# Seven block products for eight in a feed-forward up projection on TensorE

## The chip, the cores and the metric

The kernel runs on one core of a Trainium2 chip. The metric is device time in microseconds for one execution, as the median over runs. One profiled execution of the kernel before is read here. Its engines are TensorE (PE in the profile, with its weight loads as PEld), VectorE (DVE), ScalarE (ACT), GpSimd (POOL) and SyncE (SP), which only issues transfers.

## What is computed

Two transformer blocks over 1024 tokens of width 1024, in float32. The change lies in the feed-forward part of the first block, where D_FF is 2816:

```
def causal_dwconv(x, w):
    ...
    xp = jnp.pad(x, ((0, 0), (k - 1, 0), (0, 0)))
    out = xp[:, 0:t] * w[0]
    for i in range(1, k):
        out = out + xp[:, i:i + t] * w[i]
    return out

def conv_glu_ffn(h, w_up, conv_w, w_down):
    up = causal_dwconv(h @ w_up, conv_w)
    gate, val = jnp.split(up, 2, axis=-1)
    return (jax.nn.silu(gate) * val) @ w_down
...
        h = rms_norm(x, ffn_norm_g[l])
        x = x + conv_glu_ffn(h, w_up[l], ffn_conv_w[l], w_down[l])
```

So the up projection is a product of 1024 tokens x 1024 by 1024 x 5632 (2816 gate columns, then 2816 value columns), a convolution of three taps along the tokens follows, and the gated values go through a 2816 x 1024 down projection.

## The kernel before

A float32 product is made of three passes on TensorE: each operand is split into a rounded high part and a low part (`split`: ACT casts the high part at L101, DVE subtracts it at L102), and `mm3` (L124) adds high x high, high x low and low x high. Tokens lie along the free axis in two halves of 512, since one PSUM bank holds 128 x 512 floats.

**Ahead of the up projection**, `out_unit` (L960 to L964) makes 128 tokens x 512 columns of x per unit, and `Norm` normalizes each 128-token row group: `put` (L165 to L185) scales it, `turn` (L194) transposes it on PE and splits it into `hh` and `hl`, the two parts of the transposed activations. One turn is done behind each following unit, and the last one stands behind the last unit.

**The up projection** runs over 22 units `fi`. A unit is one block of 128 gate columns and one of 128 value columns. For each, `wload` brings a 1024 x 128 block of weights (`wraw`, 512 KB, SP queue) and splits it into `whi` and `wlo`; `mm3` makes 8 k-tiles x 3 passes x 2 token halves = 48 matmuls of 128x512 into `mm`, a tile of two banks, of which there are two. `up_evict` applies the convolution straight from PSUM: ACT scales (L1044), DVE adds the two shifted taps (L1045, L1046). Then ACT takes tanh (L1066), DVE makes `th` (L1067) and the gated product (L1071) in two halves, which stay in SBUF in the tiles `gg`. In unit 20 the first row of `w_down` and `gg[0][0]` are split ahead into `down0` (L1072 to L1080).

**The down projection** (L1149 to L1180) has four groups (token half j, column half c). Each runs over the 22 rows fi of `w_down`: SP loads `wr` (256 KB), ACT and DVE split it and the matching `gg` half, and PE makes 12 matmuls into four accumulators.

Instructions run on each engine in a fixed order that a scheduler lays down when the program is built: it takes what is ready by its estimate, and `high_priority` moves splits ahead. At run time each engine works through its list in order, and waits on semaphores.

Of the kernel before, what the change touches and what calls it, by code (L numbers as in the profile page):

```python
# [8 lines left out]
F32 = mybir.dt.float32  # L9
# [57 lines left out]
def kernel(ctx: ExitStack, tc: tile.TileContext, A: dict, out: bass.AP, stop=None):  # L67
# [129 lines left out]


# [4 lines left out]
    mmp = stw.enter_context(tc.tile_pool(name="mmp", bufs=2, space=PSUM))  # L203
# [724 lines left out]
    st1.close()  # L928

# [71 lines left out]
    def block2_tables(pool):  # L1001
# [3 lines left out]
        for c in range(3):  # L1005
# [30 lines left out]
        tc.keep_in_program_order(V.tensor_scalar(gq[:, 1:2], PV("qn_gain"), -(96.0 ** -0.5), None, op0=ALU.mult))  # L1036

    gg = []
    std0 = ExitStack()
    with tc.tile_pool(name="up", bufs=1) as up:  # L1040
        def up_evict(ps, ci):
            a = up.tile([128, T], F32, name="cv", bufs=3)
            w = [PV("ffn_conv_w", 2 * NF * i + ci) for i in range(3)]
            S.activation(a, ps, AF.Copy, scale=w[2])  # L1044
            V.scalar_tensor_tensor(a[:, 1:T], ps[:, 0:T - 1], w[1], a[:, 1:T], op0=ALU.mult, op1=ALU.add)  # L1045
            V.scalar_tensor_tensor(a[:, 2:T], ps[:, 0:T - 2], w[0], a[:, 2:T], op0=ALU.mult, op1=ALU.add)  # L1046
            return a
# [697 lines left out]
```

## Time and profile before

| | us |
|---|---|
| median of 3 runs | 2501.16 |
| lowest, highest | 2499.43, 2503.86 |
| the profiled execution, time | 2500.26 |
| the profiled execution, span | 2498.2 |

The span is what the profile covers; 2.06 us of the profiled execution's time lie outside it. The page gives the busy time of each engine; the windows of the trace give the same by stage, with TensorE's granted clock as a share of its full rate (1.00 is 2.4 GHz, 0.50 is 1.2 GHz); the chain of waits tells what the end of a stretch hung on.

### The profile page before, as it was taken

To read this page: it belongs to the slowest core of one execution; us is meant where nothing else is said; L and a number is where in the kernel's file an instruction comes from. 1 tells how busy PE (TensorE), PEld (TensorE's weight loads), DVE (VectorE), ACT (ScalarE), POOL (GpSimd) and SP (SyncE) were. 2 spreads that over 40 slices of the span, in tenths; PEclk is the share of its full clock that TensorE was granted. 3 is DMA by queue.
4 is the path that set the end of the run, shared out by engine and by line. 5 is a ranking of instruction groups with operands and counts; after the bars stand their busy time and mean duration, and the time that the engine had idled before them with its cause. 6 is when DMAs were issued, how large, how long until landed. Compare 5 with 4: busy or idle time off the path is not lost.

```text
span 2498.2 us, 31184 instructions
## 1 busy us (share of the span) xinstructions
PE 2401.9 (96%) x11582; PEld 1941.4 (78%) x11582; DVE 1310.4 (52%) x2247; ACT 993.0 (40%) x1869; POOL 356.9 (14%) x477
## 2 busy tenths in 40 slices
PE   6999899999999989999999999999999999999999
PEld 5887676777777767788788888888789787787787
DVE  4245754578454333444444444556665534767852
ACT  4344333322333223322222222345556634669840
POOL 0122310013232211000000000001013200126510
PEclk9999999999999999999999999999999999999999
DMA  5322115353232355611111111334532556766433
GB/s 159 93 89 79 55 55 171 133 164 121 87 110 77 116 166 175 203 64 51 45 51 51 51 43 47 123 97 135 163 118 85 147 182 178 194 184 180 128 106 137
DMA packets 272055, 288.10 MB, mean 115 GB/s; under 512 B 13968, under 2 KB 208160, under 8 KB 271904
## 3 DMA queue, kind: packets, MB, share of 16 engines
q1 hardware_dynamic: 233056, 245.81, 32.8%
q10 hardware_dynamic: 38848, 40.31, 4.8%
q8 instruction: 91, 1.49, 0.2%
q14 instruction: 60, 0.49, 0.1%
HBM read 207.31 MB, written 78.75 MB: 115 GB/s over the span
## 4 chain that ended last, share of the span: by engine, by line
PE 46%; DMA 6%; ACT 4%; DVE 3%; issue 2%; SPq 0%; POOLq 0%; ACTq 0%; POOL 0%; DVEq 0%
PE mm L124 19%; PE ip L1230 3%; DMA mr<-merged 1%; DMA wr<-in_w_in_dram 1%; PE ip L1119 1%; PE ip L1120 1%; PE ip L1121 1%; PE iq L315 1%; PE tp L331 1%; PE iq L316 1%; PE lt L1514 1%; ACT p L1518 1%; DMA zr<-in_w_in_dram 1%; PE ip L962 1%; PE ip L960 1%
## 5 line engine op out<-in xcount | busy, mean ns | idle before, releaser
L101 ACT CAST whi<-wraw 128x1024 fp32r<-128x1024 f32 (+1 forms) x138 | 121.7, 883 | 505.5 <-PE mm L124 472.1
L102 DVE TENSOR_TENSOR wlo<-wraw,whi 128x1024 fp32r<-128x1024 f32 (+1 forms) x138 | 141.8, 1031 | 330.6 <-ACT whi L101 324.2
L124 PE MATMUL mm<-hh,whi 128*128 128x512 f32 x896 | 306.7, 414 | 7.6 <-ACT th L857 6.7
L124 PE MATMUL mm<-hh,wlo 128*128 128x512 f32 x896 | 292.0, 397 | 1.3 <-DVE wlo L116 1.3
L124 PE MATMUL mm<-hl,whi 128*128 128x512 f32 x896 | 291.5, 397 | 0.0
L124 PE MATMUL mm<-h2l,whi 128*128 128x512 f32 x704 | 222.4, 389 | 0.0
L124 PE MATMUL mm<-h2h,wlo 128*128 128x512 f32 x704 | 222.1, 389 | 0.0
L124 PE MATMUL mm<-h2h,whi 128*128 128x512 f32 x704 | 222.0, 389 | 0.0
L124 PEld LDWEIGHTS mm<-hh,wlo 128*128 128x128 f32 x896 | 170.0, 190 | 41.1 <-issue 2.5
L124 PEld LDWEIGHTS mm<-hl,whi 128*128 128x128 f32 x896 | 169.1, 190 | 36.8 <-DVE hl L102 0.4
L124 PEld LDWEIGHTS mm<-hh,whi 128*128 128x128 f32 x896 | 158.6, 191 | 44.8 <-ACT th L857 8.8
L124 PEld LDWEIGHTS mm<-h2l,whi 128*128 128x128 f32 x704 | 132.1, 188 | 28.6 <-issue 1.3
L124 PEld LDWEIGHTS mm<-h2h,whi 128*128 128x128 f32 x704 | 132.1, 188 | 28.1 <-ACT whi L101 0.6
L124 PEld LDWEIGHTS mm<-h2h,wlo 128*128 128x128 f32 x704 | 132.1, 188 | 27.4
L168 POOL TENSOR_TENSOR rs<-rs,negh 128x1 f32<-128x1 f32 x32 | 19.5, 610 | 869.1 <-ACT junk L165 603.1
L1518 ACT ACTIVATE p<-p,mn 128x640 f32<-128x640 f32 (+7 forms) x128 | 99.4, 778 | 12.2 <-DVE mn L1516 11.7
L102 DVE TENSOR_TENSOR ptl<-tp,pth 128x512 fp32r<-128x512 f32 (+3 forms) x144 | 78.0, 555 | 31.6 <-ACT pth L101 30.3
L102 DVE TENSOR_TENSOR gl<-s,gh 128x512 fp32r<-128x512 f32 x87 | 60.0, 690 | 64.6 <-ACT gh L101 62.1
L101 ACT CAST gh<-s 128x512 fp32r<-128x512 f32 x87 | 53.9, 621 | 78.7 <-PE iq L1177 32.7
L101 ACT CAST pth<-tp 128x512 fp32r<-128x512 f32 (+3 forms) x144 | 67.0, 477 | 42.5 <-PE tp L331 41.2
L315 PE MATMUL iq<-pth,v 128*128 128x512 f32 x192 | 70.7, 370 | 9.2 <-DVE t L1543 4.5
L867 POOL TENSOR_TENSOR acc<-acc,pacc 128x1024 f32<-128x1024 f32 x20 | 50.8, 2539 | 184.9 <-DVE acc L862 156.2
(508 smaller groups left out, 5223.5 us busy)
## 6 DMA issues: line engine op xcount, KB each, us to landing
wraw<-in_w_in_dram SPq DMA_DIRECT2D x60, 512.0 KB, 3.9
wraw<-in_w_up_dram SPq DMA_DIRECT2D x44, 512.0 KB, 3.8
wr<-in_w_down_dram SPq DMA_DIRECT2D x87, 256.0 KB, 2.6
merged<-acc SPq DMA_DIRECT2D x28, 512.0 KB, 3.0
pacc<-merged SPq DMA_DIRECT2D x20, 512.0 KB, 4.3
x<-x ACTq DMA_DIRECT2D x16, 512.0 KB, 3.0
v2t<-vo ACTq DMA_DIRECT2D x16, 512.0 KB, 2.6
v<-v2t SPq DMA_DIRECT2D x16, 512.0 KB, 4.0
```

The lines of the kernel that those rows point to most:

```text
L101: S.copy(hi, src)
L102: (eng or V).tensor_tensor(lo, src, f(hi), op=ALU.subtract)
L124: PE.matmul(ps[:, c0 + j * 512:c0 + (j + 1) * 512], w[:, k, :], x[j][:, k, :], start=(k == 0 and w is wh and x is xh), stop=(k == nkt - 1 ...
L315: PE.matmul(po[-1][:, w], vh[:, k, :], ph_[:, w], start=(k == 0), stop=False)
L316: PE.matmul(po[-1][:, w], vh[:, k, :], pl_[:, w], start=False, stop=(k == nk - 1))
L331: PE.transpose(pt[:, i * 128:(i + 1) * 128], P[p0 + i][:, k * 128:(k + 1) * 128], ident)
L867: G.tensor_tensor(ac, ac, pa, op=ALU.add)
L960: PE.matmul(po, mh[:, k, :], wh, start=(k == 0), stop=False)
L962: PE.matmul(po, ml[:, k, :], wh, start=False, stop=(k == NK - 1))
L1119: PE.matmul(ps[:, :ncol], xh[:, k, :], wh[:, :ncol], start=(k == 0), stop=False)
L1230: PE.matmul(ps[j], w[:, k, :], x[j][:, n, :], start=(n == 0 and w is wh and x is hh), stop=(n == 7 and bool(last)))
L1518: S.activation(pr_[:, :L], pr_[:, :L], AF.Exp, scale=-1.0, bias=mn[:, c:c + 1], accum_out=self.den[:, i:i + 1])
```

## The change

The up projection's product is cut into blocks: the weights of a unit are [gate | value] by the two halves of the 1024 input rows (q = 0, 1), the activations the same two halves by the two token halves (j = 0, 1). Each of the four results (gate or value, by token half) is a sum of two block products, eight in all, each of 4 k-tiles x 3 passes = 12 matmuls of 128x512. Units 1 to 21 now use the Strassen-Winograd form: seven products of sums and differences of blocks, 84 matmuls instead of 96. Unit 0 stays plain (`plain`), in four pieces of 24 matmuls.

- The sums of activations (T1 to T4, each 128 x 2048) are made once behind the last norm turn: two subtractions on DVE, two on POOL, and six splits of 128x2048. The turn copies the transposed tile as raw float32 (`R2`) first and splits only the first token half.
- The sums of weights (S1 to S4, each 128x512) are made for each unit on POOL, in two pairs, and split as pairs (`w2`, `w3`). `w1` splits the gate block, `w4` one half of the value block.
- Each product adds up in one bank: `ac` (four banks) or `ip` (two). Three products share `c` and two share `d` in turn, and DVE evicts the partial sums (u2, e15, and the halves of `cg` and `cx`), adding an SBUF operand; ACT copies e1 and the first gate half.
- The convolution reads `cg` and `cx` from SBUF instead of PSUM. The gated product runs on POOL in one piece of 128x1024 and is written to DRAM (`gg_d`).
- The down projection loads the gated values back into SBUF, 44 loads of 256 KB, in the loop of its two groups j = 0. `down0` is gone.
- Pools are set on other sides of SBUF, the values' convolution weights are halved once (`vw`), and the tables of the second block are made piece by piece.

The core of the diff:

```
-        for fi in range(NF):
...
-            w2 = [wload(A["w_up"][:, ci * 128:(ci + 1) * 128], NK) for ci in (fi, NF + fi)]
-            ps = [mmp.tile([128, T], F32, name="mm") for _ in range(2)]
...
-            if fi == NF - 2:
...
-                    split(down0[0], down0[1], raw)
-                    split(down0[2], down0[3], gg[0][0])
+                S.copy(self.raws[q, j][:, :, s], pt)
+                if j == 0:
+                    hi, lo = self.parts[q]
+                    split(hi[:, :, s], lo[:, :, s], self.raws[q, j][:, :, s])
...
+        def sums(self):
+            (a11, a12), (a21, a22) = map(halves4, self.raw)
...
+            G.tensor_tensor(x[:, 1], a21, a22, op=ALU.add)
+            G.tensor_tensor(x[:, 0], x[:, 1], a11, op=ALU.subtract)
+            G.tensor_tensor(y[:, 0], a11, a21, op=ALU.subtract)
+            G.tensor_tensor(y[:, 1], a12, x[:, 0], op=ALU.subtract)
...
+        def product(self, acc, w, x, start):
+            (wh, wl), (xh, xl) = w, x
+            for k in range(4):
+                for n, (a, b) in enumerate(((wh, xh), (wh, xl), (wl, xh))):
+                    PE.matmul(acc, a[:, k, :], b[:, k, :], start=(start and k + n == 0), stop=(k == 3 and n == 2),
+                              skip_group_check=True)
...
+        def copies(self):
...
+                S.copy((self.v if n % 2 else self.g)[:, s], self.b[n])
+        def p1(self):
+            self.a = self.bank()
+            self.product(self.a, self.a11, B1[0], True)
+            self.e()
...
+            S.copy(self.e1, self.a)
...
+        def p6(self):
+            self.c = self.bank()
+            self.product(self.c, self.s2, T2, True)
...
+            V.tensor_tensor(self.u2, self.c, self.e1, op=ALU.add)
...
+            V.tensor_tensor(self.e15, self.d, self.e1, op=ALU.add)
+        def p7(self):
+            self.product(self.c, self.s3, T3, False)
...
+            V.tensor_tensor(self.v[:, 512:1024], self.c, self.e15, op=ALU.add)
+        def p3(self):
+            self.product(self.d, self.s4, B22, False)
+            V.tensor_tensor(self.g[:, 512:1024], self.d, self.u2, op=ALU.add)
+        def p4(self):
+            self.product(self.c, self.a22, T4, False)
+            V.tensor_tensor(self.v[:, 0:512], self.c, self.e1, op=ALU.add)
+        def conv(self, x, w):
...
+            S.activation(a, x, AF.Copy, scale=w[2])
...
+        def value(self):
+            b = self.conv(self.v, [vw[:, NF * i + self.fi:NF * i + self.fi + 1] for i in range(3)])
+            G.tensor_tensor(b, self.th, b, op=ALU.mult)
+            (nc.sync if self.fi < NF - 1 else G).dma_start(gg_d[self.fi * 128:(self.fi + 1) * 128, :], b)
...
+    V.tensor_tensor(R2[0, 0], R2[0, 1], R2[0, 0], op=ALU.subtract)
+    G.tensor_tensor(R2[0, 1], R2[1, 1], R2[0, 1], op=ALU.subtract)
+    split(*T1, R2[0, 0])
+    V.tensor_tensor(R2[1, 1], R2[1, 1], R2[0, 0], op=ALU.subtract)
+    split(*T2, R2[1, 1])
+    v.w1()
+    G.tensor_tensor(R2[1, 0], R2[1, 0], R2[1, 1], op=ALU.subtract)
+    v.sums()
+    split(*T3, R2[0, 1])
+    v.w2()
+    split(*T4, R2[1, 0])
...
+                    if j == 0:
+                        g_ = f(slot(c))
+                        nc.sync.dma_start(g_, gg_d[fi * 128:(fi + 1) * 128, c * 512:(c + 1) * 512])
+                        gg.setdefault(fi, {})[c] = g_
```

In the changed program L1219 and L1222 are the two DVE sums of activations, L1220 and L1225 the two on POOL, L1137 the four copies of unit 0's banks; L1086 to L1089 are the weight sums on POOL and L1195 the gated product there.

**Where the first Strassen unit begins, on ACT.** Before, behind the last turn come the tables, then the steady pair of a weight cast and a scaled copy:

```order
L101 CAST whi<-wraw 128x1024
L1044 ACTIVATE cv<-mm,pv 128x1024
L1066 ACT_TABLE_LOAD
L1066 ACTIVATE th<-cv 128x1024
L101 CAST whi<-wraw 128x1024
L1044 ACTIVATE cv<-mm,pv 128x1024
```

In the changed program the casts of the activation sums stand there, with the four copies of unit 0's banks (`cg`, `cx`) behind the last of them; r_7417, r_7419, r_7416 and r_7418 are the raw blocks R2[0,1], R2[1,1], R2[0,0] and R2[1,0]:

```order
L101 CAST t4h<-r_7417 128x2048
L101 CAST b2h<-r_7419 128x2048
L101 CAST t1h<-r_7416 128x2048
L101 CAST t3h<-r_7417 128x2048
L101 CAST whi<-wraw 128x1024
L101 CAST t2h<-r_7419 128x2048
L101 CAST t4h<-r_7418 128x2048
L1137 COPY cg<-ac 128x512
L1137 COPY cx<-ac 128x512
L1137 COPY cg<-ac 128x512
```

The copies that free the banks have moved behind the cast of R2[1,0], which L1225 on POOL makes.

**One unit of the up projection, on DVE.** Before, one unit is nine instructions:

```order
L102 TENSOR_TENSOR wlo<-wraw,whi 128x1024
L1045 SCALAR_TENSOR_TENSOR cv<-mm,pv,cv 128x1023
L1046 SCALAR_TENSOR_TENSOR cv<-mm,pv,cv 128x1022
L1071 SCALAR_TENSOR_TENSOR s_8298<-th,cv 128x512
L1071 SCALAR_TENSOR_TENSOR s_8299<-th,cv 128x512
L102 TENSOR_TENSOR wlo<-wraw,whi 128x1024
L1045 SCALAR_TENSOR_TENSOR cv<-mm,pv,cv 128x1023
L1046 SCALAR_TENSOR_TENSOR cv<-mm,pv,cv 128x1022
L1067 SCALAR_TENSOR_TENSOR th<-th,cv 128x1024
```

In the changed program a unit is fourteen; these are twelve in a row, from the first value half `cx` of one unit on (u_ is u2, e_ is e1 or e15; the two that follow are L1183 and L1184 on `cg`):

```order
L1178 TENSOR_TENSOR cx<-ac,e_8644 128x512
L1191 SCALAR_TENSOR_TENSOR th<-th,cv 128x1024
L102 TENSOR_TENSOR a2l<-wraw,a2h 128x512
L1183 SCALAR_TENSOR_TENSOR cv<-cx,vw,cv 128x1023
L1159 TENSOR_TENSOR u_8824<-ac,e_8782 128x512
L1184 SCALAR_TENSOR_TENSOR cv<-cx,vw,cv 128x1022
L1165 TENSOR_TENSOR e_8839<-ip,e_8782 128x512
L102 TENSOR_TENSOR ulo<-s_8849,uhi 128x1024
L102 TENSOR_TENSOR wlo<-wraw,whi 128x1024
L1170 TENSOR_TENSOR cx<-ac,e_8839 128x512
L1174 TENSOR_TENSOR cg<-ip,u_8824 128x512
L102 TENSOR_TENSOR ulo<-s_8850,uhi 128x1024
```

The convolution's taps now have two SBUF operands, and five additions that read a bank (`ac`, `ip`) have come between the splits.

**The head of the down projection, on SP's queue.** Before, three rows of `w_down` go ahead, then rows and blocks of the residual x (L1189) in turn:

```order
L1164 DMA wr<-in_w_down_dram 128x512 [waits PE_49]
L1164 DMA wr<-in_w_down_dram 128x512 x2
L1164 DMA wr<-in_w_down_dram 128x512 [waits DMAHW3_49,DVE_49]
L1164 DMA wr<-in_w_down_dram 128x512 [waits DMAHW4_49,DVE_49]
L1164 DMA wr<-in_w_down_dram 128x512 [waits DMAHW5_49,DVE_49]
L1189 DMA x_11493<-x_7408 128x1024 [waits DMAHW2_49,DVE_49]
L1189 DMA x_11495<-x_7408 128x1024 [waits PE_49]
L1164 DMA wr<-in_w_down_dram 128x512 [waits DMAHW6_49,DVE_49]
L1189 DMA x_11497<-x_7408 128x1024
```

In the changed program the loads of the gated values (L1367, gg) come in behind four blocks of x (L1394) and five rows of `w_down` (L1370), two of which wait for DVE:

```order
L1370 DMA wr<-in_w_down_dram 128x512 [waits PE_49]
L1370 DMA wr<-in_w_down_dram 128x512 [waits DMAHW1_49]
L1370 DMA wr<-in_w_down_dram 128x512 [waits DMAHW2_49]
L1394 DMA x_11861<-x_7409 128x1024 [waits DMAHW3_49,PE_49]
L1394 DMA x_11863<-x_7409 128x1024 [waits DMAHW4_49]
L1370 DMA wr<-in_w_down_dram 128x512 [waits DMAHW6_49,DMAHW0_49,DVE_49]
L1394 DMA x_11865<-x_7409 128x1024 [waits DMAHW7_49]
L1370 DMA wr<-in_w_down_dram 128x512 [waits DMAHW1_49,DVE_49]
L1394 DMA x_11867<-x_7409 128x1024
L1367 DMA s_11326<-gg 128x512 [waits DMAHW2_49]
L1367 DMA s_11350<-gg 128x512 [waits DMAHW3_49]
```

The first product of the down projection now needs the load s_11326; before, it took operands that unit 20 had split.

## Rows read from the trace of the kernel before

**Rows 1.** The page's first part: span, busy time of the engines.

```profile
span 2498.2 us, 31184 instructions
PE 2401.9 (96%) x11582; PEld 1941.4 (78%) x11582; DVE 1310.4 (52%) x2247; ACT 993.0 (40%) x1869; POOL 356.9 (14%) x477
```

**Rows 2.** Windows: PE, PEld, DVE, ACT, POOL busy; PEclk; DMA share; GB/s.

```profile
1200.00:1300.00 100.00, 100.00 (x443) 82.77 (x442) 45.76 (x42) 24.46 (x25) 0.00 (x0) 1.00 0.16 48
1600.00:1650.00 50.00, 50.00 (x221) 41.20 (x220) 26.01 (x41) 22.24 (x40) 0.00 (x0) 1.00 0.38 117
```

**Rows 3.** Chain of waits over the up projection: start, length, what.

```profile
1197.25 385.80 PE mm L124 x1701
```

**Rows 4.** Timeline where the up projection begins: start, length, engine, line.

```profile
1100.59 0.39 PE L124 MATMUL mm<-h2h,whi 128*128 128x512 f32 x1
...
1104.90 0.60 PE L194 MATMUL tp<-cv,xn 128*128 128x128 f32 x4
```

**Rows 5.** Instructions by line, up projection and out units: busy, mean ns.

```profile
L1046 DVE SCALAR_TENSOR_TENSOR cv<-mm,pv,cv 128x1022 f32<-128x1022 f32 x42 | 53.8, 1281 | 1.5
L102 DVE TENSOR_TENSOR wlo<-wraw,whi 128x1024 fp32r<-128x1024 f32 x42 | 51.5, 1225 | 213.0 <-ACT whi L101 213.0
...
L101 ACT CAST whi<-wraw 128x1024 fp32r<-128x1024 f32 x42 | 44.3, 1054 | 276.1 <-PE mm L124 276.1
L1071 DVE SCALAR_TENSOR_TENSOR s<-th,cv 128x512 f32<-128x512 f32 x42 | 27.2, 689 | 0.7
...
L964 DVE TENSOR_TENSOR x<-x,ip 128x512 f32<-128x512 f32 x16 | 11.0, 685 | 18.3 <-PE ip L962 17.9 <-DMA x<-in_x_dram 0.4
...
L101 ACT CAST h2h<-tp 128x512 fp32r<-128x512 f32 x16 | 8.9, 582 | 16.8 <-PE tp L194 16.7
```

**Rows 6.** Instructions by line on POOL, whole span.

```profile
L867 POOL TENSOR_TENSOR acc<-acc,pacc 128x1024 f32<-128x1024 f32 x20 | 50.8, 2539 | 184.9 <-DVE acc L862 156.2 <-issue 25.1 <-PE tp L741 3.6
L1545 POOL TENSOR_TENSOR zz<-zz,rdb 128x512 f32<-128x512 f32 x16 | 20.6, 1289 | 219.3 <-DMA rdb<-rd 200.4 <-DVE mn L1516 11.4 <-DMA zz<-z 7.6
```

**Rows 7.** Timeline of DVE, two stretches with POOL at work.

```profile
835.82 0.42 DVE L794 COPY z<-py 64x256 f32<-64x256 f32 x1 [1.05 <-PE py L792]
...
904.72 1.22 DVE L102 TENSOR_TENSOR wlo<-wraw,whi 128x1024 fp32r<-128x1024 f32 x1
906.01 3.36 DVE L102 TENSOR_TENSOR l<-wr,h 128x512 fp32r<-128x512 f32 x2
```

**Rows 8.** Timeline of POOL in the same two stretches.

```profile
834.40 2.38 POOL L867 TENSOR_TENSOR acc<-acc,pacc 128x1024 f32<-128x1024 f32 x1 [22.17 <-DVE acc L862]
...
904.89 3.33 POOL L867 TENSOR_TENSOR acc<-acc,pacc 128x1024 f32<-128x1024 f32 x1 [14.57 <-DVE acc L862]
913.21 2.39 POOL L867 TENSOR_TENSOR acc<-acc,pacc 128x1024 f32<-128x1024 f32 x1 [5.00 <-issue]
```

**Rows 9.** Timeline of PE: two stretches behind idle time (in brackets).

```profile
876.20 1.97 PE L832 MATMUL tp<-cv,ytk 128*128 128x128 f32 x8 [6.43 <-DVE ytk L825]
...
925.07 0.73 PE L124 MATMUL mm<-hh,whi 128*128 128x512 f32 x2 [3.51 <-ACT th L857]
```

**Rows 10.** Windows behind those two idle times, as in rows 2.

```profile
876.00:878.00 2.00, 1.80 (x9) 1.80 (x10) 1.28 (x2) 0.00 (x0) 0.00 (x0) 0.50 0.68 245
...
880.00:882.00 2.00, 2.00 (x6) 1.52 (x6) 0.00 (x0) 0.00 (x0) 0.42 (x1) 0.52 0.33 129
882.00:884.00 2.00, 2.00 (x11) 1.60 (x10) 0.00 (x0) 0.00 (x0) 0.00 (x0) 1.00 0.29 27
...
928.00:930.00 2.00, 2.00 (x7) 1.52 (x6) 0.32 (x1) 0.00 (x0) 2.00 (x1) 0.57 0.82 230
```

**Rows 11.** Timeline where the down projection begins.

```profile
1582.87 0.39 PE L124 MATMUL mm<-h2h,wlo 128*128 128x512 f32 x1
...
1583.10 0.39 PE L1176 MATMUL ip<-d,d 128*128 128x512 f32 x1
...
1583.94 1.29 DVE L102 TENSOR_TENSOR gl<-s,gh 128x512 fp32r<-128x512 f32 x2
```

**Rows 12.** Transfers of the down projection (KB each, us to landing); a busy window.

```profile
wr<-in_w_down_dram SPq DMA_DIRECT2D x53, 256.0 KB, 2.6
x<-x SPq DMA_DIRECT2D x4, 512.0 KB, 8.7
...
1040.00:1042.00 2.00, 2.00 (x10) 1.64 (x9) 1.53 (x3) 0.00 (x0) 0.00 (x0) 1.00 1.00 354
```

More of the change, by code (lines that the diff above doesn't have):

```diff
@@ new lines @@
+    us = [Unit(fi) for fi in range(NF)]
+    u, v = us[0:2]
+    u.load()
+    u.w1()
+    upp = stu.enter_context(tc.tile_pool(name="upp", bufs=1, space=PSUM))
+    u.plain(0)
+    u.wv()
+    v.load()
+    last_turn()
+    sto.close()
+    up = stu.enter_context(tc.tile_pool(name="up", bufs=1, side="right", reuse_waits="tile"))
+    tpool = stu.enter_context(tc.tile_pool(name="tpool", bufs=1, side="right", reuse_waits="tile"))
+    T4, T1, T2, T3, B22 = [[tpool.tile([128, 4, 512], F32R, name=f"{n}{e}") for e in "hl"] for n in ("t4", "t1", "t2", "t3", "b2")]
@@ new lines @@
+    B12 = T4
+    u.plain(1)
+    split(*B12, R2[0, 1])
+    split(*B22, R2[1, 1])
+    u.plain(2)
+    u.plain(3)
+    V.tensor_tensor(R2[0, 0], R2[0, 1], R2[0, 0], op=ALU.subtract)
[8 more added lines that the diff above has]
+    v.w2()
@@ new lines @@
+    for n in range(1, NF):
+        u, v, w = us[n], us[n + 1] if n < NF - 1 else None, us[n - 1]
+        u.p1()
+        if n == 1:
+            u.w4()
+        if v:
+            v.load()
+        if n > 1:
+            w.p4()
+            w.value()
+            u.w3()
+        if tables:
+            next(tables, None)
+        if n == 1:
+            u.p2()
+            u.c11()
+            w.gate()
+            w.value()
+        u.p6()
+        u.p5()
+        if v:
+            v.w1()
+            v.w4()
+            v.sums()
+        if n > 1:
+            u.p2()
+            u.c11()
+        else:
+            u.w3()
+        u.p7()
+        if v:
+            v.w2()
+        u.p3()
+        u.gate()
+        if n == 4:
+            tables = block2_tables(stu.enter_context(tc.tile_pool(name="tb", bufs=1)))
+        if tables:
+            next(tables, None)
@@ L1081, with slot @@
+    u.p4()
+    u.value()
+    for _ in tables:
+        pass
+    stu.close()
     st2.close()
     stw.close()
+    slots = st3.enter_context(tc.tile_pool(name="slots", bufs=NF, reuse_waits="tile"))
+    def slot(j, ncol=512):
+        return slots.tile([128, 512], F32R, name=f"s{j}")[:, :ncol]
+    gg = {}
     x3_d = dram.tile([T, D], F32, name="x3")
     sth = ExitStack()
-    h3pool = sth.enter_context(tc.tile_pool(name="h3pool", bufs=1, reuse_waits="tile"))
+    h3pool = sth.enter_context(tc.tile_pool(name="h3pool", bufs=1, side="right", reuse_waits="tile"))
@@ L1148 @@
     nm, xs = None, []
-    with tc.tile_pool(name="dw", bufs=1, reuse_waits="tile") as dw:
+    with tc.tile_pool(name="dw", bufs=1, side="right", reuse_waits="tile") as dw:
         rows_ = [[lambda k=k: Wc.append(row2(dw, A["w_in_2"], 0, 2048, 416, k, 3)) for k in range(NK)]
@@ L1598 @@
     stf = ExitStack()
[L1599 removed]
+    fo = stf.enter_context(tc.tile_pool(name="fo", bufs=1, side="right", reuse_waits="tile"))
     for h in range(NG, 16):
@@ L1628 @@
     sta.close()
-    with tc.tile_pool(name="fp", bufs=1, side="right", reuse_waits="tile") as fp:
+    with tc.tile_pool(name="fp", bufs=1, reuse_waits="tile") as fp:
         def out_x(t, c):
```

177 lines of the change are left out of this document (114 added, 63 removed).

## The prediction

> **What bounds the kernel now.** I read the page first: TensorE is busy for 2401.9 of 2498.2 us [rows 1], so the kernel is as long as its matmuls unless a stage says otherwise. The windows say it for the stage in question: from 1200 to 1300 us PE is busy for 100.00 of 100.00 us at a granted clock of 1.00, with DVE at 45.76, ACT at 24.46 and POOL at 0.00 [rows 2]. The chain of waits agrees: one piece of 385.80 us with 1701 matmuls and no wait in it [rows 3], which is 385.80 / 1701 = 0.2268 us for one 128x512 matmul. The reader should see two things there: the stage pays for each matmul that goes, and the other engines' work costs nothing as long as one unit of it fits under one unit of matmuls. The edges are tight too. The up projection follows the last out unit at 1100.59, with the last transposes woven in at 1104.90 [rows 4], and the down projection's first matmul starts 0.23 us behind the last one of the up projection [rows 11]. Every gap that the change opens at an edge is therefore added in full.
>
> **Part 1, the matmuls.** Before, 22 units of 96 make 2112. After, unit 0 has 96 and 21 units have 84, 1860 in all: 252 fewer. That the pass now adds up in one bank, where before two banks took turns, costs nothing by the down projection, which has one bank at a time and runs 221 matmuls in 50.00 us, 0.2262 each [rows 2]. 252 x 0.2268 = **-57.1 us**. All of it lies on the path.
>
> **Part 2, a unit in the steady state.** PE needs 84 x 0.2268 = 19.05 us. DVE has four splits or sums of 128x1024 with two SBUF operands (two pairs of S, w1, th: 4 x 1.225), four taps (4 x 1.28), one split of 128x512 (0.69) and five evictions (5 x 0.69) [rows 5]: 4.90 + 5.12 + 0.69 + 3.45 = 14.16. Instructions in a row overlap by some 0.09 (two of 128x512 take 1.29 together [rows 11], one takes 0.69), so 14 of them need about 12.9. ACT has some 8.5 and doesn't matter. POOL has four sums of 128x512 (4 x 1.289 [rows 6]) and a product of 128x1024 (2.39 undisturbed [rows 8]): 7.55.
>
> These can't all run side by side. At 904.89 POOL's sum ran for 3.33 us instead of 2.39, and two DVE splits that need 1.29 together took 3.36, ending as POOL ended [rows 7, 8]: with two SBUF operands on DVE, one engine stood while the other worked. At 835.82 a DVE copy out of PSUM inside a POOL sum took its 0.42 [rows 7, 8]. So I put the nine DVE instructions with two SBUF operands (about 9.9) and POOL's 7.55 in series, 17.5, and let the five evictions (3.0) run beside POOL. Laying out one unit in the engines' order by these prices, with PE in the order P1, P4 of the unit before, P6, P5, P2, P7, P3, DVE ends its unit near 17.8 of 19.05. The evictions that PE waits for have 2.5 to 4 us to spare, so I take **0** per unit. With nothing beside anything it is 12.9 + 7.55 = 20.45, which is 1.4 over, times 21 units = +29. The layout is nearer to the first, since the evictions do lie beside POOL's work in it; for the range I allow +10.
>
> The Trainium skill, "SBUF — State Buffer", section "Who interferes with whom", states this as a rule: DVE and GpSimd share a port pair under an exclusive lock, a DVE instruction with two SBUF inputs contends with a GpSimd instruction that reads SBUF and the later one blocks fully, and one with at most one SBUF input, outside the two-port modes, doesn't contend. The trace agrees, 3.36 against 1.29 and 0.42 unstretched. The rule speaks against this change, which moves the taps from PSUM to SBUF and gives POOL new work: without it the sum would be about 12 us lower (rival A), by it the sum is as here.
>
> **Part 3, the start.** Unit 0's first piece of 24 matmuls ends at 1100.59 + 5.44 = 1106.03. Eight transposes follow, 0.60 for four [rows 4], and a copy of 0.58 [rows 5], so the raw block is there near 1107.15. From there PE has three more pieces and P5 of unit 1: 1.2 + 3 x 5.44 + 2.72, until 1125.9. Beside that the activation sums are made in 128x2048, which no row has: I take twice the 1024 rows less an overlap of 0.09, 2.36 on DVE [rows 5] and 4.69 on POOL [rows 8], and 2.1 on ACT [rows 5]. By the order: L1219 and two splits on DVE until 1114.2; L1220 on POOL, which DVE's next split waits out, until 1118.9; t1l and L1222 until 1123.6; t3l until 1126.0; L1225 on POOL until 1130.7; its cast on ACT until 1132.8, and behind that cast in ACT's list the copy that frees a bank for P1 of unit 1, 0.6. P1 starts near 1133.4, so PE idles 7.5. The clock then falls: behind 6.43 us of idle time the granted clock stayed at 0.50 to 0.52 until about 882, 5.8 us, and behind 3.51 us for some 3 us [rows 9, 10]. 5.8 us at half rate lose 2.9. DVE is by then behind: t2l, t4l, two weight splits, unit 0's taps and th stand ahead of u2 of unit 1, some 15.6 us from 1130.7, and POOL's sums of unit 2 cut in for 1 to 2 more, so u2 comes near 1148; PE asks for it, behind P1, P2 and P6, near 1144.5 less what the clock lost in them: a wait of about 4. I add 1.4 for P4 of unit 1 and 2.5 in unit 2 until the lists have caught up. Sum **+18**. From below: if POOL holds up nobody, P1 waits for 4.2 us and the clock costs 1.5, together 5.7. From above 21. I take 18, since rows 7 and 8 show the blocking itself.
>
> **Part 4, the head of the down projection.** Before, there was no gap [rows 11]. After, SP's list has three rows of w_down, two blocks of x, then w_down rows that wait for DVE, and only then the first gated load. Let E be the last up matmul. Its second value half is evicted until E + 1.2, ACT scales until 2.4, and the tap follows until 3.65; the split dwl that frees a w_down buffer stands behind it (4.3), the next behind th (6.0). SP issues the first gated load near E + 6.9. A row of 256 KB takes 2.6 us to land, but x blocks took 8.7 in this stretch [rows 12], and 512 KB of x are ahead in the queues, so I say E + 10.5 to 11. The cast (0.62) and the wait behind it put the first matmul at E + 11.7, and its low part a little later: idle about 12, with bounds of 9 (nothing ahead of it) and 15 (SP held once more). The clock costs 1.5 to 2.9 by the rows above. Sum **+14.5**, 11 to 18. Unit 20's splits that go (`down0`) lay beside matmuls and give nothing.
>
> **Part 5, the rest of the down projection.** While c = 0, SP loads 22 w_down rows and 44 gated pieces: about 3.5 x 256 KB in each 2.72 us, 330 GB/s. The busiest window moved 354 at a share of 1.00 [rows 12]. It fits, barely; the loads ahead give some room. I take **+1**, 0 to 5. The gated writes (22 x 512 KB) and the pools' new sides lie beside matmuls: DMA share there is 0.16 [rows 2].
>
> **Sum.** -57.1 + 0 + 18 + 14.5 + 1 = -23.6. On the profiled execution's own 2500.26 that is 2476.7. The median of the runs stands 0.9 higher, so I say **2477**. Its own range: best ends -57.1 + 5.7 + 11 + 0 = -40, worst -57.1 + 10 + 21 + 18 + 5 = -3; together hardly ever, so 2462 to 2494.
>
> **Rivals.** A: POOL and DVE hardly block each other at the start. For it: rows 7 and 8 are two places only. Against: both engines stretched there at once. The start costs 6, so the time is 2465.
>
> B, the other side: a DVE split that is blocked by POOL also holds the evictions queued behind it, so DVE and POOL take strict turns. A unit then is 20.45 to 20.6, 21 x 1.4 to 1.55 = +29 to +33: 2506 to 2510, say 2508, slower than before. For it: DVE's list is in order and POOL is asked for in mid-unit. Against: the layout leaves 1.2 us, and PE's products need the evictions 2.5 us late at the earliest. It decides from 1.15 us per unit over 19.05 on.
>
> C: half of that, units of 19.5 to 20: +10 to +20, 2487 to 2497.
>
> D: the first gated load is hidden after all, because the DVE waits ahead of it come earlier than in my layout: 9 less at the end, 2468.
>
> **How the numbers follow.** Forecast 0.5, A 0.17, B 0.10, C 0.13, D 0.10. The predicted time is the forecast's, 2477. A and D lie below it, C above, so 2460 to 2497 holds these and most of C and leaves out B and a little on the low side: under 2 in 10. A measurement of this kernel tells about 0.2% from no change, 5 us: faster ends at 2496, slower starts at 2506. Forecast, A and D are faster, and most of C: 0.84. Same takes the end of C and the low end of B: 0.06. Slower is the rest of B: 0.10.
>
> **What would show it.** In the changed profile: a PE unit of 19.0 us from about 1160 on with no idle time ahead of P7, P3 and P4, and DVE groups of the taps near 1.3 us with stretched ones beside POOL; PE idle 6 to 8 us near 1126 with an ACT copy L1137 as what ended it; PE idle 9 to 15 us at the first L13xx matmul with the cast of a gated piece as what ended it, and a granted clock near 0.5 behind both gaps. The prediction is wrong if units take over 19.5 us (B, C), if the start's gap is under 4 us (A), or if the down projection starts within 4 us of E (D).

## The result

The changed kernel takes 2474.44 us (median of 4 runs, 2472.34 to 2480.85), the kernel before 2501.91 (2499.43 to 2503.86): a ratio of 0.9895 with a 95% interval of 0.9873 to 0.9917, 1.05% faster. The forecast was 2477, with a range of 2460 to 2497.

The page of the changed kernel's profile (span, then busy time by engine), against [rows 1]:

```profile
span 2470.9 us, 31217 instructions
...
PE 2350.9 (95%) x11330; PEld 1899.5 (77%) x11330; DVE 1468.2 (59%) x2351; ACT 1067.2 (43%) x1971; POOL 586.8 (24%) x586
```

PE has lost 252 matmuls and 51 us of busy time; DVE has gained 158 us and POOL 230. Windows of the same trace (columns as in [rows 2]): the start, the steady units, then the head of the down projection:

```profile
1130.00:1140.00 10.00, 10.00 (x35) 8.04 (x35) 8.88 (x8) 6.11 (x9) 3.33 (x2) 0.75 0.37 108
...
1200.00:1300.00 100.00, 100.00 (x435) 80.10 (x434) 83.73 (x76) 42.06 (x48) 52.56 (x26) 1.00 0.26 82
...
1558.00:1560.00 2.00, 1.57 (x4) 1.24 (x5) 1.33 (x2) 1.00 (x2) 0.00 (x0) 0.50 1.03 415
1560.00:1562.00 2.00, 2.00 (x7) 1.56 (x6) 0.00 (x0) 0.00 (x0) 0.00 (x0) 0.57 1.06 407
```

In the steady units PE is still busy for 100.00 of 100.00 us, with DVE at 83.73 and POOL at 52.56 beside it. Nearly all that was paid lies at the two ends. The timeline of PE shows it; these are all of its waits of over 0.4 us from the first up matmul to the down projection:

```profile
1128.94 0.79 PE L1113 MATMUL ac<-b0h,whi 128*128 128x512 f32 x1 [5.82 <-ACT cg L1137]
...
1146.53 0.50 PE L1113 MATMUL ac<-t3h,uhi 128*128 128x512 f32 x1 [2.91 <-DVE u L1159]
...
1152.48 0.50 PE L1113 MATMUL ac<-t4h,a2h 128*128 128x512 f32 x1 [0.88 <-DVE cx L1170]
...
1164.24 0.50 PE L1113 MATMUL ac<-t3h,uhi 128*128 128x512 f32 x1 [0.51 <-DVE u L1159]
...
1174.89 0.50 PE L1113 MATMUL ac<-t4h,a2h 128*128 128x512 f32 x1 [2.19 <-DVE cx L1170]
...
1558.43 0.79 PE L1381 MATMUL ip<-dwh,gh 128*128 128x512 f32 x1 [15.32 <-ACT gh L101]
```

The table splits profiled executions into stages, and is used from here on. "Up" runs from the start of the first up matmul to that of the last, "gap" from there to the first down matmul, "down" to the last one. Times are us; the last column is the median of the runs.

| kernel | up | gap | down | median |
|---|---|---|---|---|
| before | 482.3 | 0.2 | 249.5 | 2501.91 |
| changed | 445.1 | 15.7 | 248.4 | 2474.44 |
| changed_again | 444.2 | 16.0 | 250.2 | 2472.23 |
| start_sums_on_dve | 440.8 | 16.0 | 248.3 | 2472.94 |
| residual_loads_late | 444.2 | 11.9 | 250.9 | 2473.84 |
| gated_loads_ahead | 444.5 | 10.9 | 263.5 | 2487.64 |
| pieces_and_rows_in_turn | 444.3 | 4.9 | 255.3 | 2468.03 |
| both_mended | 440.6 | 4.9 | 255.9 | 2465.76 |
| two_steps_ahead | 440.7 | 0.2 | 253.6 | 2461.17 |
| seventh_product_twice | 497.7 | 15.8 | 249.9 | 2527.82 |
| seventh_product_out | 411.8 | 15.7 | 250.5 | 2443.50 |
| pool_sums_twice | 495.4 | 15.8 | 249.5 | 2532.95 |

What lies ahead of "up" and behind "down" is the same work in all the changed ones, yet the first up matmul starts anywhere from 1095.7 to 1102.6 us and the stretch behind takes 662.5 to 667.9. The kernel before ran beside each set at 2499.2 to 2501.9. A span or a median therefore resolves some 3 us between two of these kernels, a stage about 1.

### The profile page after: what moved, and what is told of

Same layout as the page of the kernel before. It is cut to its first block, busy times and chain, and to the rows that moved or that the text cites. A ratio compares the mean times of both kernels' runs of the same rounds, so it can differ in the third digit from the quotient of the medians.

```text
span 2470.9 us, 31217 instructions
## 1 busy us (share of the span) xinstructions
PE 2350.9 (95%) x11330; PEld 1899.5 (77%) x11330; DVE 1468.2 (59%) x2351; ACT 1067.2 (43%) x1971; POOL 586.8 (24%) x586
## 4 chain that ended last, share of the span: by engine, by line
PE 46%; DMA 5%; DVE 4%; ACT 3%; issue 2%; POOL 0%; SPq 0%; POOLq 0%; ACTq 0%; DVEq 0%
PE ac L1113 11%; PE ip L1113 4%; PE ip L1435 2%; DMA zr<-in_w_in_dram 1%; PE iq L335 1%; PE ip L1324 1%; PE tp L351 1%; PE ip L1325 1%; PE ip L1326 1%; DMA mr<-merged 1%; PE iq L336 1%; PE lt L1719 1%; PE ip L1383 1%; PE ip L1381 1%; PE ip L1382 1%
## 5 line engine op out<-in xcount | busy, mean ns | idle before, releaser
L101 ACT CAST whi<-wraw 128x1024 fp32r<-128x1024 f32 (+1 forms) x117 | 99.6, 852 | 261.4 <-PE mm L124 203.6
L102 DVE TENSOR_TENSOR wlo<-wraw,whi 128x1024 fp32r<-128x1024 f32 (+1 forms) x117 | 117.0, 1003 | 116.3 <-ACT whi L101 109.7
L168 POOL TENSOR_TENSOR rs<-rs,negh 128x1 f32<-128x1 f32 x32 | 19.5, 612 | 386.4 <-DVE rs L167 386.4
L101 ACT CAST uhi<-s 128x1024 fp32r<-128x1024 f32 x42 | 44.1, 1052 | 118.4 <-PE ip L1113 80.7
L102 DVE TENSOR_TENSOR ulo<-s,uhi 128x1024 fp32r<-128x1024 f32 x42 | 88.5, 2109 | 5.2 <-ACT uhi L101 5.2
L1195 POOL TENSOR_TENSOR cv<-th,cv 128x1024 f32<-128x1024 f32 x22 | 53.1, 2414 | 130.5 <-issue 92.4
L351 PE MATMUL tp<-cv,p 128*128 128x128 f32 x432 | 71.1, 275 | 2.4 <-DVE ptl L102 2.3
L1750 POOL TENSOR_TENSOR zz<-zz,rdb 128x512 f32<-128x512 f32 x16 | 20.6, 1290 | 214.7 <-DMA rdb<-rd 198.0
L336 PE MATMUL iq<-ptl,v 128*128 128x512 f32 x192 | 68.6, 363 | 0.2 <-DVE ptl L102 0.2
```

The costliest lines, as they stand in the source:

```text
L101: S.copy(hi, src)
L102: (eng or V).tensor_tensor(lo, src, f(hi), op=ALU.subtract)
L336: PE.matmul(po[-1][:, w], vh[:, k, :], pl_[:, w], start=False, stop=(k == nk - 1))
L351: PE.transpose(pt[:, i * 128:(i + 1) * 128], P[p0 + i][:, k * 128:(k + 1) * 128], ident)
L1195: G.tensor_tensor(b, self.th, b, op=ALU.mult)
```

## The experiments

The theory is the prediction's: PE alone sets the steady unit; DVE and POOL take turns; the start pays because the sums of activations pass through both, and the head of the down projection because of SP's list. Three runs test the steady unit, one the start, four the head, and both_mended joins two of these.

### The matmuls: the seventh product twice

```
         def p7(self):
             self.product(self.c, self.s3, T3, False)
+            self.product(self.c, self.s3, T3, False)
```

> Edit: the twelve matmuls of P7 run twice in each of the 21 units, so that a unit has 96 matmuls again as before the change (the result is not the reference's: P7 counts double). Theory (the steady units are bound by TensorE alone, 0.2268 us a matmul): 252 more matmuls cost 57.1 us, 2531, and the waits of the first two units shrink by a few us, so 2526 to 2531. Rival (other engines set part of the unit's length): less than 50 us.

Measured: 2527.82 us (2527.12 to 2528.52), ratio to before 1.011 (1.009 to 1.013). Two pieces of the chain of waits, one unit apart (start, length, what):

```profile
1332.66 8.25 PE ac L1113 x36
...
1354.51 8.25 PE ac L1113 x36
```

A unit takes 21.85 us where the changed kernel's takes 19.13: 2.72 for twelve matmuls, 0.2267 each. "Up" grows by 52.6 and not by 57.1: of the waits listed above, those of 0.88, 0.51 and 2.19 us are gone, filled by the longer units. So the matmul term stands at its full price. It also shows what the rest of the change costs: with as many matmuls as before, the kernel is 28 us slower than before on the same chip (2500.21).

### The other engines' unit: the seventh product out, and POOL's sums twice

```
         def p7(self):
-            self.product(self.c, self.s3, T3, False)
```

> Edit: the twelve matmuls of P7 are left out in each of the 21 units, with all else in its place (the result is not the reference's: one product is missing). PE then needs 72 x 0.2268 = 16.33 us a unit. Theory of the prediction (DVE's two-operand instructions and POOL's take turns, a unit of other work ends near 17.8 of 19.05 us): a unit falls only to about 17.8, 21 x 1.3 = 27 us less than the changed kernel, 2447. Rival (DVE and POOL overlap and leave PE alone to set the unit): 252 matmuls fewer, 57 us less, 2417.

Measured: 2443.5 us (2439.4 to 2447.59), 28.7 less than the changed kernel on the same chip; "up" falls by 32.4. The timeline of PE, at the same place of two units in a row, and a window:

```profile
1350.87 0.50 PE L1113 MATMUL ip<-b2h,uhi 128*128 128x512 f32 x1 [0.72 <-DVE e L1165]
...
1368.33 0.50 PE L1113 MATMUL ip<-b2h,uhi 128*128 128x512 f32 x1 [0.74 <-DVE e L1165]
```

```profile
1300.00:1400.00 100.00, 96.31 (x417) 77.63 (x416) 95.95 (x80) 45.15 (x52) 64.97 (x30) 1.00 0.27 87
```

A unit is 17.46 us, not the 16.33 that PE needs; DVE is busy for 95.95 of 100 us and PE waits for its eviction. So the unit of the other engines is 17.5 us, as the theory said (17.8), and the rival falls. The changed kernel has 1.7 us of 19.13 to spare.

```
         def sums(self):
             ...
-            G.tensor_tensor(x[:, 1], a21, a22, op=ALU.add)
-            ...
+            for _ in range(2 if self.fi > 2 else 1):
+                G.tensor_tensor(x[:, 1], a21, a22, op=ALU.add)
+                ...
```

> Edit: from the third unit of the value and gate blocks on, POOL makes each of its four weight sums twice (the same values into the same places), 5.16 us of work more in a unit. Theory (DVE with two SBUF operands and POOL take turns; without P7 a unit was 17.47 us, set by DVE): a unit needs 17.5 + 5.2 = 22.6 us instead of 19.13, and 19 units cost some 65 us more than the changed kernel, about 2538. Rival (POOL, busy for 12.7 of 19.1 us, runs beside DVE): no change, 2474.

Measured: 2532.95 us (2532.68 to 2533.21), ratio to before 1.0131 (1.011 to 1.0152). PE now waits for u2 in nearly every unit (first and last of the steady ones; the window below runs from one to the other):

```profile
1218.79 0.50 PE L1114 MATMUL ac<-t3h,uhi 128*128 128x512 f32 x1 [1.56 <-DVE u L1160]
...
1570.57 0.50 PE L1114 MATMUL ac<-t3h,uhi 128*128 128x512 f32 x1 [1.39 <-DVE u L1160]
```

```profile
1218.79:1570.57 351.78, 323.59 (x1351) 257.75 (x1351) 329.17 (x228) 126.68 (x145) 287.30 (x145) 0.97 0.24 73
```

Sixteen units take 351.8 us, 22.0 each, against 22.6 expected. POOL got 5.16 us of work more, and was idle for 9 us of each unit before; DVE's own instructions are the same, yet its busy time rises from 16.0 us a unit (83.73 in 100 us) to 20.6 (329.17 / 16). So POOL's sums don't run beside DVE's instructions with two SBUF operands here, and the rival falls. The 22.0 isn't a pure price of turns, though: of the 2.9 us more per unit, 1.8 are PE's idle time (351.78 less 323.59, over 16), and the granted clock, 0.97 over the stretch, accounts for some 0.6 more. The kernel would have lost its gain from about 1.3 us more per unit on (27.5 us over 21 units).

### The start: the sums of activations on DVE

```
-    G.tensor_tensor(R2[0, 1], R2[1, 1], R2[0, 1], op=ALU.subtract)
+    V.tensor_tensor(R2[0, 1], R2[1, 1], R2[0, 1], op=ALU.subtract)
...
-    G.tensor_tensor(R2[1, 0], R2[1, 0], R2[1, 1], op=ALU.subtract)
+    V.tensor_tensor(R2[1, 0], R2[1, 0], R2[1, 1], op=ALU.subtract)
```

> Edit: the two 128x2048 sums of activations that the change gave to POOL (L1220, L1225) are made on DVE. Theory (DVE with two SBUF operands and POOL take turns, and the copy that frees a bank for P1 of unit 1 stands in ACT's list behind a cast that waits for L1225): in the changed kernel each of these sums stood DVE still for about 4.4 us; on DVE it costs 2.2. L1225 then ends near 1121 instead of 1126.5, P1 of unit 1 starts 4 to 5 us earlier (its 5.82 us of idle time become 1 to 2), and the sum u2 of unit 1 comes 4 to 9 us earlier. The time falls by 4.5 to 9 us, to about 2467. Rival (the two engines don't hold each other up, POOL is only slow): DVE's list gets 4.4 us longer, u2 of unit 1 comes later, and the time stays or rises by up to 4 us.

First the changed kernel itself. Timelines of DVE, POOL and ACT at its start:

```profile
1108.79 2.28 DVE L102 TENSOR_TENSOR b2l<-r,b2h 128x2048 fp32r<-128x2048 f32 x1
1110.99 6.69 DVE L102 TENSOR_TENSOR t1l<-r,t1h 128x2048 fp32r<-128x2048 f32 x1
...
1122.01 6.60 DVE L102 TENSOR_TENSOR t2l<-r,t2h 128x2048 fp32r<-128x2048 f32 x1
```

```profile
1108.95 6.58 POOL L1220 TENSOR_TENSOR r<-r,r 128x2048 f32<-128x2048 f32 x1 [8.47 <-DVE t4l L102]
1119.96 6.50 POOL L1225 TENSOR_TENSOR r<-r,r 128x2048 f32<-128x2048 f32 x1 [4.43 <-DVE r L1222]
```

```profile
1126.50 1.90 ACT L101 CAST t4h<-r 128x2048 fp32r<-128x2048 f32 x1 [4.67 <-POOL r L1225]
1128.31 0.58 ACT L1137 COPY cg<-ac 128x512 f32<-128x512 f32 x1
```

L1220 is ready at 1108.95 but waits for b2l, which is in its 2.28 us; then t1l waits for L1220, so that both last some 6.6 us where a free one takes 2.28 on DVE and, by the difference, about 4.4 on POOL (an estimate: no free sum of this size ran there). The same again with L1225 and t2l. The cast of its result and the copy behind it end PE's wait of 5.82 us.

With the sums on DVE, the PE timeline of the experiment:

```profile
1128.32 0.50 PE L1113 MATMUL ac<-b0h,whi 128*128 128x512 f32 x1 [1.41 <-ACT cg L1137]
...
1134.46 0.50 PE L1113 MATMUL ac<-b1h,whi 128*128 128x512 f32 x1 [1.99 <-ACT e L1146]
...
1142.65 0.50 PE L1113 MATMUL ac<-t3h,uhi 128*128 128x512 f32 x1 [0.83 <-DVE u L1159]
1154.42 0.79 PE L1113 MATMUL ac<-t4h,a2h 128*128 128x512 f32 x1 [4.45 <-DVE cx L1170]
```

The wait of 5.82 is 1.41, as the theory said, and "up" is 3.4 to 4.3 us shorter, where 4.5 to 9 were expected: part of it moved on, since P2 now waits 1.99 for a copy on ACT and P4 4.45 for cx. The four waits add up to 8.7 us, against 12.3 in the changed kernel. The median, 2472.94 us (ratio 0.9892, 0.9877 to 0.9906), can't be told from the changed kernel's; the stage can. The rival, by which the time would stay or rise, doesn't give the shorter stage.

### The head: the queue in front of the first gated piece

SP's own timeline in the changed kernel, where the last up matmul starts at 1542.71 (start, time over the group, what), and the piece of the chain of waits:

```profile
1543.14 0.80 SPq L1394 DMA_DIRECT2D x<-x  x2
1547.39 0.33 SPq L1370 DMA_DIRECT2D wr<-in_w_down_dram  x1
1548.63 0.32 SPq L1394 DMA_DIRECT2D x<-x  x1
1549.12 0.33 SPq L1370 DMA_DIRECT2D wr<-in_w_down_dram  x1
1549.50 0.43 SPq L1394 DMA_DIRECT2D x<-x  x1
1549.97 11.17 SPq L1367 DMA_DIRECT2D s<-gg  x12
```

```profile
1549.97 7.76 DMA s<-gg
```

The first gated piece is issued 7.3 us behind the start of the last up matmul and lands 7.76 later. (The 9.6 us and the gap of 18.1 us in the next two expectations, and the 11 us for a row in a later one, count from some 2 to 4 us earlier; from the start of the last up matmul they are 7.3, 15.7 and 7.1.)

```
-                        nc.sync.dma_start(x2, x1_d[...])
+                        tc.keep_in_program_order(nc.sync.dma_start(x2, x1_d[...]))
```

> Edit: the four 512 KB loads of the residual x keep their place in the program, behind the group's products, so that they no longer stand ahead of the first gated loads in SP's list; nothing else. In the changed kernel the first gated piece was issued 9.6 us behind the last up matmul and took 7.8 us to land. Theory (2 MB of x ahead in the same queues make it land late): it is issued 0.5 to 1 us earlier and lands in 3 to 4 us, the down projection starts 4 to 5 us earlier, and the time falls to about 2470. Rival (the DVE waits ahead of it in SP's list are all that counts): the time falls by 0.5 to 1 us.

Measured: 2473.84 us (ratio 0.9894, 0.9874 to 0.9915).

```profile
1554.42 0.80 PE L1381 MATMUL ip<-dwh,gh 128*128 128x512 f32 x1 [11.49 <-ACT gh L101]
```

The gap falls from 15.32 to 11.49. SP's timeline of this run has the piece's issue 6.8 us behind the start of the last up matmul, against 7.3:

```profile
1549.33 8.01 SPq L1367 DMA_DIRECT2D s<-gg  x12
```

So it landed some 4.4 us later (1554.42 less the cast of 0.63), not 7.76, and 3.4 of the 3.8 us are landing time: the 2 MB of x ahead of it. The rival (0.5 to 1) falls for the gap; in the median nothing of it can be told.

```
+        for fi in range(8):
+            gload(fi, 0)          # kept in the program's order, ahead of the rows
...
+                    if c == 0 and fi == 8:
+                        ...       # the four x2 loads, kept there
```

> Edit: eight gated pieces are loaded ahead of the first rows of w_down in SP's list, rows and pieces then keep the order of the program, and the x loads come at the ninth step of each first group. No wait on DVE stands ahead of the first gated piece then, only the last gated write of SP, some 6 us before the last up matmul. Theory (the gap of 18.1 us at the head of the down projection is this queue): what is left is the casts of the first piece and row behind the last unit's taps on ACT and DVE, 6 to 7 us behind the last up matmul; the time falls by 11 to 12 us, to about 2463. Rival (the splits behind the last unit, or the transfers, would take the place of the wait): the gap stays above 12 us and the time falls by less than 6 us.

Measured: 2487.64 us (2484.69 to 2488.72; ratio 0.9948, 0.9933 to 0.9962), 13 us slower than the changed kernel: neither theory. Timelines of PE and of SP, and between them a piece of the chain of waits at the first gap:

```profile
1557.99 0.79 PE L1393 MATMUL ip<-dwh,gh 128*128 128x512 f32 x1 [10.51 <-ACT dwh L101]
...
1720.53 0.79 PE L1393 MATMUL ip<-dwh,gh 128*128 128x512 f32 x1 [5.14 <-ACT dwh L101]
```

```profile
1549.88 3.87 DMA fg<-in_final_norm_g_dram
```

```profile
1706.56 9.18 SPq L1387 DMA_DIRECT2D x<-x  x4
1715.83 33.94 SPq L1376 DMA_DIRECT2D wr<-in_w_down_dram  x14
```

The gap fell by 4.8 us and changed its owner, from the gated piece (gh) to the row (dwh) that now came behind eight pieces. Their number alone didn't hold the row up: by the profile's waits SP stood 8.4 us at one of the eight and 2.8 at another, each time until a load from ACT's queue had landed (the chain shows the second, of `final_norm_g`, which ACT issues behind the last unit's tanh). Then the edit made a wait of its own: the x loads of the second token half need buffers that the first half's last step frees, and the rows of w_down that the third group needs stood behind them in SP's list. PE's waits at 1708 to 1721 add up to 9.0 us (1.83, 1.54, 0.45 and 5.14), and the granted clock was 0.50 from 1712 to 1725; the two account for most of the 13 to 15 us more in "down".

> Edit: none, the changed kernel again, beside the two that follow on the same chip. Every theory: 2474 us within 3.

Measured: 2472.23 us (2469.8 to 2478.06). The next two ran beside it.

```
-                        nc.sync.dma_start(g_, gg_d[...])
+                        (tc.keep_in_program_order if c == 0 and fi < 22 else id)(nc.sync.dma_start(g_, gg_d[...]))
...
-                    nc.sync.dma_start(raw, A["w_down"][...])
+                    (tc.keep_in_program_order if j + c == 0 and fi < 22 else id)(nc.sync.dma_start(raw, A["w_down"][...]))
...
+                    if j + c == 0 and fi == 8:
+                        xloads(j, tc.keep_in_program_order)
```

> Edit: in the first group of the down projection SP's list takes a gated piece and a row of w_down in turn, in the order of the program, so that four pieces and three rows stand ahead of the first wait on DVE; the x loads of the first token half come at the ninth step of that group, those of the second keep their free place. It mends two things that gated_loads_ahead brought in: rows behind eight pieces (the first row was issued 11 us behind the last up matmul), and x loads of the second half ahead of rows that the third group waited for (5.14 us and more at 1706 to 1720). Theory (the gap is what SP's list puts ahead of the first piece and row): the first down matmul comes 6 to 7 us behind the last up matmul instead of 15.3, set by the casts behind the last unit's taps, and nothing is given back later: 8 to 10 us less than the changed kernel, 2465. Rival (the transfers themselves are late, two streams into SBUF at once): the gap stays above 11 us and the gain under 5 us.

Measured: 2468.03 us (2467.63 to 2471.94; ratio 0.9875, 0.9858 to 0.9891), 4.2 less than changed_again.

```profile
1545.69 0.79 PE L1390 MATMUL ip<-dwh,gh 128*128 128x512 f32 x1 [4.52 <-ACT dwh L101]
1550.55 0.80 PE L1391 MATMUL ip<-dwl,gh 128*128 128x512 f32 x1 [4.07 <-DVE dwl L102]
```

The first matmul comes 4.9 us behind the last one, not 15.7, so the gap was SP's list. But half of the 11 us went to what follows, and "down" is 5 to 7 us longer. One wait I had not counted: the low part of the first row is split on DVE behind the last unit's taps, 4.07 us. Nor does the clock's fall go away: the granted clock is 0.51 over the ten us from the first down matmul on, where the same ten us have 0.84 in the changed kernel and 0.72 in changed_again.

> Edit: pieces_and_rows_in_turn and start_sums_on_dve together. Theory (the two places have nothing to do with each other): the gains add up, 8 to 10 and 4, so 12 to 14 us less than the changed kernel, 2461. Rival (they overlap, or the later stage gives one back): no more than 8 us.

Measured: 2465.76 us (2463.4 to 2470.44; ratio 0.9863, 0.9848 to 0.9878), 6.5 less than changed_again. By its size that is the rival's. But in the stages the two edits do add up ("up" 440.6, "gap" 4.9); the sum is half of what was expected for the reasons just given, the wait behind the mended one and the clock, and not because the two overlap.

```
+    for fi in range(2):
+        raw = wpool.tile([128, NK, 128], F32, name="wraw").rearrange("p a b -> p (a b)")
+        tc.keep_in_program_order(nc.sync.dma_start(raw[:, 0:512], A["w_down"][fi * 128:(fi + 1) * 128, 0:512]))
+        tc.keep_in_program_order(nc.sync.dma_start(raw[:, 512:1024], gg_d[fi * 128:(fi + 1) * 128, 0:512]))
+        ...
+        with tc.high_priority():
+            split(hi, lo, raw)
     u.p4()
     u.value()
+    ...                           # the first two steps' 24 matmuls
```

> Edit: both_mended, and the operands of the down projection's first two steps are loaded into the two weight buffers that the last unit leaves free and split there, ahead of that unit's taps on ACT and DVE; the gated write of the last but one unit goes by POOL's queue too, so that these loads don't wait for it in SP's list. Theory (in both_mended the first down matmul came 4.5 us late by the cast of its row, and the first low part 4.07 us later by its split, both behind the last unit's taps): the first 24 matmuls follow the last up matmul within 1 us and last 5.4 us, the third step's splits come 8 us behind the last up matmul, so 2 to 3 us of idle time are left and little of the clock's fall: 6 to 9 us less than both_mended, 2458. Rival (the splits that are moved ahead hold up the last unit's evictions, or its tail ends later by as much): less than 3 us.

Measured: 2461.17 us (2460.24 to 2464.41; ratio 0.9848, 0.9833 to 0.9863).

```profile
1539.76 0.40 PE L1113 MATMUL ac<-t4h,a2l 128*128 128x512 f32 x1
1539.99 0.39 PE L1293 MATMUL ip<-whi 128*128 128x512 f32 x1
...
1549.56 0.80 PE L1411 MATMUL ip<-dwl,gh 128*128 128x512 f32 x1 [3.73 <-DVE dwl L102]
```

The first down matmul follows without a gap, and one wait of 3.73 us is left, where 2 to 3 were expected. From the last up matmul to the last down matmul it takes 253.8 us, both_mended 260.8: 7.0 less, as expected. The medians, from two chips, differ by 4.6. Of the kernels that leave nothing out this is the fastest, 1.5% under the kernel before.

## Why the prediction was right

The spans differ by 27.3 us, and the steps of the prediction add up to that as follows (us; measured from the stages above):

| step | forecast | measured | worked out as |
|---|---|---|---|
| part 1, matmuls | -57.1 | -57.1 | 252 x 0.2267, by seventh_product_twice |
| part 2, steady units | 0 | +1.7 | 21 x (19.13 - 19.05) |
| part 3, start | +18 | +18.2 | 445.1 - 482.3 + 57.1 - 1.7 |
| part 4, head of down | +14.5 | +17.1 | 15.7 - 0.2, and 1.6 for the clock |
| part 5, rest of down | +1 | -2.7 | 248.4 - 249.5, less that 1.6 |
| ahead of and behind the stages | 0 | -4.5 | spread between runs |
| sum | -23.6 | -27.3 | |

The 1.6 us of the clock are what PE's 3.57 busy us between 1558 and 1562 lost at 0.50 and 0.57.

**Part 1** was right to the digit: one bank at a time costs nothing.

**Part 2** was right in its mechanism and near in its size. DVE and POOL do take turns in the steady state. By line, from 1200 to 1500 us (mean ns of one):

```profile
L102 DVE TENSOR_TENSOR ulo<-s,uhi 128x1024 fp32r<-128x1024 f32 x31 | 67.2, 2167 | 3.9 <-ACT uhi L101 3.9
L1195 POOL TENSOR_TENSOR cv<-th,cv 128x1024 f32<-128x1024 f32 x16 | 38.8, 2423 | 81.1 <-issue 81.1
L1089 POOL TENSOR_TENSOR s<-wraw,s 128x512 f32<-128x512 f32 x16 | 36.3, 2272 | 0.0
...
L1184 DVE SCALAR_TENSOR_TENSOR cv<-cg,pv,cv 128x1022 f32<-128x1022 f32 x15 | 33.0, 2198 | 0.5
...
L1191 DVE SCALAR_TENSOR_TENSOR th<-th,cv 128x1024 f32<-128x1024 f32 x16 | 19.6, 1226 | 9.1 <-ACT th L1190 9.1
...
L1087 POOL TENSOR_TENSOR s<-s,wraw 128x512 f32<-128x512 f32 x15 | 19.4, 1290 | 1.2
```

A tap that meets a POOL sum (L1184 on cg) takes 2.20 us instead of 1.28 [rows 5], and the sum 2.27 instead of 1.29 [rows 6]; where nothing meets, th takes 1.23 and the sum of L1087 1.29. The 2.17 of ulo is a mean of two: the split behind POOL's product (L1195) takes 3.10 us in most units, the other 1.23. The layout's 17.8 us per unit is 17.5 by seventh_product_out. Rival B (strict turns, 20.5) fell, and the evictions show why: L1170 and L1178 run while POOL is at work and keep their 0.69 us, as the layout had it. Rival C (19.5 to 20) fell by the 19.13. The 0.08 us that a unit is longer than its matmuls was not foreseen; no run here tells its cause.

**Part 3** came out at 18.2 for 18, but its pieces differ. The first wait was 5.82 for 7.5, just under the 6 to 8 that were to show it, since POOL's sums took 4.4 for 4.69 and each of the DVE ones 2.28 for 2.36, and since PE's own pieces in the forecast add up to 1126.3 and not to 1125.9; then 2.91 for 4, 0.88 for 1.4, and 0.51 + 2.19 for 2.5: 12.3 us of idle time for 15.4. The clock took more than its 2.9: a granted clock of 0.75 from 1130 to 1140 is 2.5, another 0.5 were lost from 1128.94 to 1130, and it fell a second time behind the wait at 1174.89, 1.7 us (0.57 from 1176 to 1180). So errors of both signs met, and that 18.2 stands beside 18 is luck. The wait of 2.19 us also has a source that the layout left out: right ahead of the cx that ended it, DVE's list has some 4 us of small instructions of the second block's tables (1168.92 to 1174.16). No run moves them, so their share isn't shown. Rival A needed POOL not to stand DVE still; start_sums_on_dve and the rows of 6.69 and 6.58 us exclude it.

**Part 4** had the right mechanism and the wrong size: the issue of the first gated piece came where the layout put it (6.9 us behind the end of the last up matmul, in the forecast and measured), but it took 7.76 us to land and not 3.6 to 4. Without the 2 MB of x ahead it took 4.4 (residual_loads_late), so they are nearly the whole of the difference; what the rows and further pieces in flight add was not separated. The idle time of 15.3 lies just above the bound of 15. Rival D (hidden after all) fell. What the prediction didn't see is that a second wait of 4 us stood behind this one, the split on DVE: the forecast didn't need it, but the attempts to mend the gap did.

**Part 5** was taken as a cost and is none that can be told: "down" lies between 248.3 and 250.5 in the five other kernels with the same list, with the fall of the clock in it, against 249.5 before; the -2.7 of the table is the low end of that. The rate that I took for the limit, 354 GB/s, isn't one: 415 GB/s were moved at 1558.

So the forecast is 2.6 us above the result, less than the spread of the parts that didn't change. That the result lies in the range follows from the steps; that it lies so near the forecast is in part luck, since parts 4 and 5 were off by 3 and 4 us with opposite signs.

## What to carry to other kernels

Cutting the matmuls of a PE-bound stage pays in full as long as the other engines' unit, counted with the instructions that exclude each other in series, stays under PE's; here 17.5 of 19.1 us. What a restructured stage costs is at its two ends: lay out the first unit and the last in each engine's order, and read what stands ahead of the one load or copy that PE waits for. When one such wait is mended, the next stands close behind it, so list the second and third before putting a price on the repair.

## What the runs showed of the hardware

With two SBUF operands on DVE, an instruction and one of POOL's wait for each other whole, in both directions: a 2.28 us split took 6.69 behind a sum of POOL's, and that sum 6.58 behind a split. The Trainium skill ("SBUF — State Buffer", section "Who interferes with whom") calls it an exclusive lock, and the traces agree. What I had not expected is that in the steady state three of POOL's four sums are hit in every unit (2.13 to 2.27 for 1.29), so that the two lists interlock one instruction at a time.

The length of a gap alone doesn't tell whether the clock falls. Behind PE's wait of 2.91 us at 1146.53 the granted clock stayed at 1.00, and behind one of 2.19 at 1174.89 it was 0.50 (windows of the changed kernel):

```profile
1147.00:1150.00 3.00, 3.00 (x15) 2.45 (x14) 3.00 (x2) 1.05 (x1) 1.41 (x1) 1.00 0.60 199
...
1174.00:1176.00 2.00, 1.11 (x5) 0.93 (x6) 1.46 (x6) 1.99 (x5) 0.00 (x0) 1.00 0.00 0
1176.00:1178.00 2.00, 2.00 (x7) 1.53 (x6) 2.00 (x2) 1.47 (x2) 0.71 (x1) 0.50 0.00 0
```

A load of 256 KB that landed in 2.6 us in the kernel before [rows 12] took 7.76 us behind 2 MB in the same queue.
